# Impulse responses of a state-space layer from the outputs' powers, asked for five steps ahead

## The chip, the cores and the metric

One core of one Trainium2 chip runs one program. The metric is the time of one execution on the device, in microseconds (us), lower is better. Five engines matter: PE multiplies matrices (its weight loads are a row of their own, PEld), DVE is the vector engine, ACT the scalar engine, POOL a second vector engine (GpSimd), SP issues the transfers of weights.

## The reference

Three layers of a language model follow each other on 256 tokens of width 1024: a gated delta rule block with a dense feed-forward, an S5 block with a mixture of experts, and a block with pooling and neighbourhood attention. Only the S5 mixer is touched here. It is a diagonal complex state-space layer with 64 groups of 16 channels and 64 states per group:

```
u = x @ w_in
a_bar = exp(lam * dt)                       # one complex number per group and state
b_bar = ((a_bar - 1) / lam) * (b_re + i b_im)
h[t] = a_bar * h[t-1] + b_bar @ u[t]        # per group
y[t] = Re(c @ h[t]) + d_skip * u[t]
hid = gelu(y);  val, gate = split(hid @ w_glu);  out = val * sigmoid(gate)
```

Before it stands a layer norm, and after it another one and the mixture of experts.

## The kernel before

**Weights.** All weight matrices are streamed. SP loads raw pieces (`wr`), ACT copies a piece rounded to the fast matmul type (`wh`, line 290), DVE subtracts to get the rest (`wl`, line 292), and `mm3` (lines 336 to 338) makes each product of three matmuls.

**The S5 stage in blocks.** The 1024 channels are eight blocks k of 128 channels, that is of eight groups. Time is cut into 64 chunks of four steps (`CH = 4`). The chunk's own inputs reach its outputs through an impulse response of four taps, a 128 by 128 matrix per tap (`BD`, masked to the 16 by 16 diagonal squares with `bd16`). What came earlier reaches it through the states at the chunk's start. Real and imaginary parts lie in the two halves of the 128 partitions.

**Four kinds of work per block.** `maps(k)` makes the block's matrices: it transposes B (input vectors times powers 0 to 3 of a_bar) into `BT` (lines 1258 and 1259), multiplies each of the four powers in B with the output vectors CX to get the taps (`pk`, line 1265), masks them on DVE into `BD` (line 1267), and then has POOL write the output vectors times powers 1 to 4 over B, in place (`C`, lines 1275 to 1277: product, product, sum). `states(k)` turns the inputs by chunks (1286, 1291), multiplies with `BT` (`px`, 1301), and computes the 64 chunk states: products with the phases CC and SS on POOL (1308) and DVE (1309, 1310), a sum (1312), a scan (1313), and the products back on POOL (1317) and DVE (1318, 1319); line 1323 writes the states H over CC. `outputs(k)` multiplies H with C (`pyi`, 1335), adds the taps (`yp`, 1344) and the turned states (1346), adds the skip (1348, DVE), applies gelu (1350, ACT) and splits the result `hid` (330 on ACT, 331 on DVE). The products with `w_glu` (`po`) take `hid` block by block.

**The order of the work.** These parts are generators. `spawn(gen, lag)` queues one to go on after `lag` ticks; `tick` is called after each quarter of a weight piece, so four ticks are one block. Where a generator yields a number, it goes on that many ticks later; `S5L` holds these lags (`per=4`: a new block each four ticks, `m=1` and `mb=2` for maps). `flow` spawns states, maps and outputs at fixed ticks. The maps of blocks 0 and 1 are run at once, before the second half of the layer norm's result is turned to features (`to_features`: transposes at line 832, copies at 837 and 838). The tile framework then orders each engine's instructions; each engine works its list in order.

**Buffers.** `BD` of blocks 0 and 1 has its own two buffers, that of later blocks takes one of three slots of `BDs`. `bx` and `by`, the scaled input vectors (lines 1179 to 1188), share one temporary tile that is gone after B is built.

Of the kernel before, what the change touches and what calls it, by code (L numbers as in the profile page):

```python
# [11 lines left out]
F32 = mybir.dt.float32  # L12
# [4 lines left out]
ALU = mybir.AluOpType  # L17
# [22 lines left out]
BUFS = 5  # L40
EXTRA = 2
LAG = dict(nb=6, d=5, dp=4, n=1, rk=3, ks=4, kp=4, inv=7, i0=3, iy=8, i1=2, i2=1, lv=4, rq=4, qs=8, qp=2, v=2)
S5L = dict(per=4, s0=3, m=1, o=0, mb=2, a=2, b=2, c=2, d=4, e=2, f=1, g=1, ct=4, gt=4, keep=2)
MO = dict(d=3, t=2, b=5, a=2, sc=1)
WARM = dict(a=12, b=9, c=20, e=5, f=0)
MAGIC = 12582912.0
CH = 4
# [156 lines left out]
class Kern:  # L204
# [890 lines left out]
    def s5_tables(self, P, Pt):  # L1095

        nc, a = self.nc, self.a
        TT, TS, STT = nc.vector.tensor_tensor, nc.vector.tensor_scalar, nc.vector.scalar_tensor_tensor
        G = nc.gpsimd
        AR = P.tile([128, CH + 1, 64], F32, name="AR")  # L1100
        AI = P.tile([128, CH + 1, 64], F32, name="AI")
        nAI = P.tile([128, CH + 1, 64], F32, name="nAI")
# [2 lines left out]
        CC = P.tile([128, 64, NJ], F32, name="CC")  # L1105
        SS = P.tile([128, 64, NJ], F32, name="SS")
        CX = P.tile([128, 64, 16], F32, tag="CX", name="CX")
        self.s5t = (AR, AI, nAI, rad, B, CC, SS, CX)
        flat = B.rearrange("p k g c n -> p (k g c n)")
        wt, rbx, rby = (flat[:, n * 1024:n * 1024 + 1024].rearrange("p (g c) -> p g c", c=16) for n in (0, 2, 3))  # L1110

# [64 lines left out]
        TS(nfi, fi, -1.0, None, op0=ALU.mult)  # L1176
        yield 2
        wide = lambda v: v.unsqueeze(2).to_broadcast([128, 64, 16])
        bxy = Pt.tile([128, 2, 64, 16], F32, tag="gb", name="bxy")
        bx, by = bxy[:, 0], bxy[:, 1]  # L1180
        TT(bx, rbx, wide(fr), op=ALU.mult)
        TT(wt, rby, wide(fs), op=ALU.mult)
        yield 2
# [49 lines left out]
    def s5(self, tables):  # L1233
# [1 line left out]
        ctx = ExitStack()  # L1235
        P = ctx.enter_context(tc.tile_pool(name="s5", bufs=1))
        P2 = ctx.enter_context(tc.tile_pool(name="s52", bufs=2))
        AR, AI, nAI, rad, B, CC, SS, CX = self.s5t
        TT, TS, STT = nc.vector.tensor_tensor, nc.vector.tensor_scalar, nc.vector.scalar_tensor_tensor
        GT = nc.gpsimd.tensor_tensor  # L1240
        MM, TR = nc.tensor.matmul, nc.tensor.transpose
# [10 lines left out]

        def maps(k):

            BT = P2.tile([128, 4, 128], F32, tag="BT", name="BT", bufs=2)
            pt = self.bank("pbt", k < 2).rearrange("p (i f) -> p i f", i=4)
            for i in range(4):
                TR(pt[:, i, :], B[:, k, 2 * i:2 * i + 2].rearrange("p g c n -> p (g c n)"), ident)
            nc.scalar.activation(BT, pt, AF.Copy)
            bts[k] = BT  # L1260
            yield S5L["mb"]
            BD = P2.tile([128, CH, 128], F32, tag="BD", name="BD") if k < 2 else BDs[:, k % 3]
            pk = self.bank("pk", k < 2).rearrange("p (n f) -> p n f", n=CH)
            for n in range(CH):
                MM(pk[:, n, :], lhsT=B[:, k].rearrange("p g c n -> p (g c) n")[:, :, n],
                   rhs=CX[:, 8 * k:8 * k + 8, :].rearrange("p g c -> p (g c)"), start=True, stop=True)
            TT(BD, pk, bd16[:, None, :].to_broadcast([128, CH, 128]), op=ALU.mult)
            bds[k] = BD

            C = B[:, k].rearrange("p g c n -> p (g c n)").rearrange("p (g o c) -> p g o c", g=8, o=CH)  # L1270
            w = P2.tile([128, 8, CH, 16], F32, tag="cw", name="cw", bufs=1)
            g = slice(8 * k, 8 * k + 8)
            pw = lambda v: v[:, 1:CH + 1, g].rearrange("p n g -> p g n").unsqueeze(3).to_broadcast([128, 8, CH, 16])
            vec = lambda v: v[:, g, None, :].to_broadcast([128, 8, CH, 16])
            GT(C, pw(AR), vec(CX), op=ALU.mult)
            GT(w, pw(nAI), vec(CY), op=ALU.mult)
            GT(C, C, w, op=ALU.add)

        def states(k):

# [78 lines left out]
            nc.scalar.activation(uT[:, 0:4, 1:, js].rearrange("p k o j -> p k j o"),  # L1359
                                 self.turn4(f, 4).rearrange("p k (j o) -> p k j o", o=CH), AF.Copy)  # L1360
        for k in range(2):
            for _ in maps(k):
                pass
        nc.gpsimd.memset(R[:, :, 0], 0.0)
        self.to_features(self.src(1), 1)
        for t in range(2):
# [675 lines left out]
```

## Time and profile before

| | |
|---|---|
| runs shown: median (lowest to highest of 3) | 1286.02 us (1283.82 to 1287.36) |
| the profiled execution's own time | 1287.1 us |
| its span in the profile | 1285.3 us |
| busy share of the span: PE, PEld, DVE, ACT, POOL | 96%, 83%, 80%, 57%, 22% |
| granted TensorE clock, mean | 0.983 |
| S5 stage, from the last feed-forward product to the last gelu | about 405 to 532 us |

The page's busy shares are averages over stages with different limits. The stage touched here lasts about a tenth of the span, and what holds it up is read from the timelines of its engines. A row's duration runs from the engine's start on the instruction to its end, so time in which an instruction has started but is held up lies inside its duration. Consecutive rows of an engine overlap by some tens of nanoseconds.

### The profile page before, as it was taken

The numbers are of one execution on the slowest core, as the hardware profiler recorded it, in microseconds if no ns is written. First come the engines' busy times: TensorE is split into PE (matmuls) and PEld (weight loads), VectorE is DVE, ScalarE is ACT, GpSimd is POOL, SyncE is SP. The second block draws the span as 40 slices with busy tenths as digits, with TensorE's granted clock in tenths as the row PEclk, the third lists the DMA queues.
The fourth block names the chain that finished last, engine by engine and source line by source line (L and its number), as shares of the span: only waits on it lengthen the run. The fifth ranks groups of instructions, "written<-read, shape, count | busy, mean of one in ns | idle before, by whom it ended". The sixth has DMA issues, their size and how long they took to land. (4 is left out here: it accounts for less than half of the span.)

```text
span 1285.3 us, 19687 instructions
## 1 busy us (share of the span) xinstructions
PE 1229.9 (96%) x7579; PEld 1062.8 (83%) x7579; DVE 1031.8 (80%) x1507; ACT 732.3 (57%) x1086; POOL 280.1 (22%) x279
## 2 busy tenths in 40 slices
PE   8999998997999899889999999999999899999997
PEld 7999986997998777758888888888877677999886
DVE  6778879999767888678998999899979785766553
ACT  5744454442443653458777776867767465655442
POOL 2322001039996565110000000000002091000000
PEclk8998999999999999989999999999999899999999
DMA  8344224444644400337999989989977553545551
GB/s 330 132 140 140 78 88 162 153 176 163 244 177 159 147 34 34 124 130 269 343 343 329 341 316 372 331 319 374 346 294 301 185 184 131 194 171 193 189 186 51
DMA packets 44949, 269.18 MB, mean 209 GB/s; under 512 B 8880, under 2 KB 9280, under 8 KB 17968
## 3 DMA queue, kind: packets, MB, share of 16 engines
q1 hardware_dynamic: 40320, 257.12, 54.5%
q10 hardware_dynamic: 4336, 10.19, 2.3%
q8 instruction: 62, 1.02, 0.3%
q0 software_dynamic: 192, 0.54, 0.1%
q14 instruction: 39, 0.32, 0.1%
HBM read 266.51 MB, written 1.31 MB: 208 GB/s over the span
## 5 line engine op out<-in xcount | busy, mean ns | idle before, releaser
L292 DVE TENSOR_TENSOR wl<-wr,wh 128x1024 fp32r<-128x1024 f32 (+1 forms) x380 | 461.7, 1233 | 131.3 <-ACT wh L290 129.3
L290 ACT ACTIVATE wh<-wr 128x1024 fp32r<-128x1024 f32 (+2 forms) x390 | 391.2, 1025 | 233.1 <-PE po L338 84.9
L338 PE MATMUL pup<-wh,xg 128*128 128x512 f32 (+1 forms) x384 | 145.1, 378 | 3.4 <-PEq L1666 2.9
L337 PE MATMUL pup<-wl,xg 128*128 128x512 f32 (+1 forms) x384 | 146.3, 381 | 0.1
L336 PE MATMUL pup<-wh,xg 128*128 128x512 f32 (+1 forms) x384 | 146.1, 380 | 0.0
L292 DVE TENSOR_TENSOR wl<-wx,wh 128x1024 fp32r<-128x1024 f32 (+2 forms) x111 | 124.3, 1153 | 10.6 <-ACT wh L290 9.1
L290 ACT ACTIVATE wh<-wx 128x1024 fp32r<-128x1024 f32 (+1 forms) x112 | 104.9, 980 | 9.9 <-PE pup L338 5.9
L338 PE MATMUL p<-x,wl 128*128 128x256 f32 x320 | 91.6, 287 | 6.6 <-DVE wl L292 6.6
L292 POOL TENSOR_TENSOR wl<-wx,wh 128x1024 fp32r<-128x1024 f32 x1 | 2.5, 2478 | 409.8 <-ACT wh L290 409.8
L336 PE MATMUL p<-x,wh 128*128 128x256 f32 x320 | 91.3, 285 | 0.2 <-ACT s L994 0.2
L337 PE MATMUL p<-x,wh 128*128 128x256 f32 x320 | 91.0, 285 | 0.0
L338 PEld LDWEIGHTS pup<-wh,xg 128*128 128x128 f32 x384 | 72.6, 189 | 14.9 <-issue 3.3
L337 PEld LDWEIGHTS pup<-wl,xg 128*128 128x128 f32 x384 | 72.7, 189 | 13.8 <-DVE wl L292 3.5
L336 PEld LDWEIGHTS pup<-wh,xg 128*128 128x128 f32 x384 | 72.6, 189 | 10.9 <-issue 0.2
L337 PE MATMUL pdn<-wl,eh 128*128 128x512 f32 x176 | 70.0, 398 | 0.8 <-DVE wl L292 0.8
L336 PE MATMUL pdn<-wh,eh 128*128 128x512 f32 x176 | 69.8, 397 | 0.0
L338 PE MATMUL pdn<-wh,eh 128*128 128x512 f32 x176 | 69.5, 395 | 0.0
L338 PEld LDWEIGHTS p<-x,wl 128*128 128x128 f32 x320 | 61.8, 194 | 8.1 <-DVE wl L292 8.0
L336 PE MATMUL pm<-x,wh 128*128 128x256 f32 x224 | 63.5, 283 | 0.0
L338 PE MATMUL pm<-x,wl 128*128 128x256 f32 x224 | 63.4, 283 | 0.0
L337 PE MATMUL pm<-x,wh 128*128 128x256 f32 x224 | 63.4, 283 | 0.0
L336 PEld LDWEIGHTS p<-x,wh 128*128 128x128 f32 x320 | 62.0, 194 | 0.6 <-ACT s L994 0.4
(561 smaller groups left out, 3096.0 us busy)
## 6 DMA issues: line engine op xcount, KB each, us to landing
wr<-w_e SPq DMA_DIRECT2D x59, 1024.0 KB, 6.8
wx<-w_e SPq DMA_DIRECT2D x37, 1024.0 KB, 6.8
wr<-w_f SPq DMA_DIRECT2D x33, 1024.0 KB, 4.8
wr<-w_e SPq DMA_DIRECT2D x29, 768.0 KB, 5.1
wr<-w_up SPq DMA_DIRECT2D x16, 1024.0 KB, 4.6
wr<-w_dn SPq DMA_DIRECT2D x16, 1024.0 KB, 4.7
wx<-w_e SPq DMA_DIRECT2D x19, 768.0 KB, 6.0
wr<-w_glu SPq DMA_DIRECT2D x8, 1024.0 KB, 4.5
```

The lines of the kernel that those rows point to most:

```text
L290: self.hi = nc.scalar.activation(hi[:, :w], src, AF.Copy)
L292: self.los[self.n_split] = eng.tensor_tensor(lo[:, :w], src, hi[:, :w], op=ALU.subtract)
L336: mm(out, lhsT=l1, rhs=r1, start=start, stop=False)
L337: mm(out, lhsT=l1, rhs=r2, start=False, stop=False)
L338: self.mm = mm(out, lhsT=l2, rhs=r1, start=False, stop=stop)
```

## The change

The taps are computed from other operands. Tap n is the output vectors times power n times the input vectors. Before, the power was taken from B (stationary operand: every fourth element of B, four loads). Now the stationary operand is `bx`, the input vectors at power 0, contiguous and the same for all taps; the moving operand is CX for tap 0 and the first three powers of C for taps 1 to 3, in one matmul of 384 columns. So the taps now need C, and C is written over B as soon as B has been transposed. The second half of `maps` comes five ticks after the first in place of two. The first halves of blocks 0 and 1 still run at the stage's start, their second halves are spawned with lags of 10 and 13 ticks. All blocks take a slot of `BDs`, and `bx` gets a tile of its own that lives through the stage.

```diff
-S5L = dict(per=4, s0=3, m=1, o=0, mb=2, a=2, ...
+S5L = dict(per=4, s0=3, m=1, m0=10, o=0, mb=5, a=2, ...
...
+        bx = P.tile([128, 64, 16], F32, name="bx")
...
-        bxy = Pt.tile([128, 2, 64, 16], F32, tag="gb", name="bxy")
-        bx, by = bxy[:, 0], bxy[:, 1]
+        by = Pt.tile([128, 2, 64, 16], F32, tag="gb", name="by")[:, 0]
...
             nc.scalar.activation(BT, pt, AF.Copy)
             bts[k] = BT
-            yield S5L["mb"]
-            BD = P2.tile([128, CH, 128], F32, tag="BD", name="BD") if k < 2 else BDs[:, k % 3]
-            pk = self.bank("pk", k < 2).rearrange("p (n f) -> p n f", n=CH)
-            for n in range(CH):
-                MM(pk[:, n, :], lhsT=B[:, k].rearrange("p g c n -> p (g c) n")[:, :, n],
-                   rhs=CX[:, 8 * k:8 * k + 8, :].rearrange("p g c -> p (g c)"), start=True, stop=True)
-            TT(BD, pk, bd16[:, None, :].to_broadcast([128, CH, 128]), op=ALU.mult)
-            bds[k] = BD
...
             GT(C, pw(AR), vec(CX), op=ALU.mult)
             GT(w, pw(nAI), vec(CY), op=ALU.mult)
             GT(C, C, w, op=ALU.add)
+            yield S5L["mb"]
+            BD = BDs[:, k % 3]
+            pk = self.bank("pk").rearrange("p (n f) -> p n f", n=CH)
+            first = bx[:, g, :].rearrange("p g c -> p (g c)")
+            MM(pk[:, 0, :], lhsT=first, rhs=CX[:, g, :].rearrange("p g c -> p (g c)"), start=True, stop=True)
+            MM(pk[:, 1:, :].rearrange("p n (g c) -> p n g c", g=8), lhsT=first,
+               rhs=C[:, :, 0:CH - 1, :].rearrange("p g o c -> p o g c"), start=True, stop=True)
+            TT(BD, pk, bd16[:, None, :].to_broadcast([128, CH, 128]), op=ALU.mult)
+            bds[k] = BD
...
         for k in range(2):
-            for _ in maps(k):
-                pass
+            m = maps(k)
+            next(m)
+            self.spawn(m, S5L["m0"] + 3 * k)
```

How this moves instructions is seen in the program's order on three engines. The line numbers of the changed kernel differ a little: its 1268, 1269 and 1270 are the three operations on C (1275, 1276 and 1277 before), 1278 is the mask of the taps (1267 before), and from `states` on each line stands two further down.

POOL, two neighbouring blocks in the middle of the stage. Before:

```order
L1308 TENSOR_TENSOR p<-X,CC 128x512
L1317 TENSOR_TENSOR p<-X,CC 128x512
L1275 TENSOR_TENSOR B<-AR,CX 128x512
L1322 MEMSET CC 128x8
L1277 TENSOR_TENSOR B<-B,cw 128x512
L1276 TENSOR_TENSOR cw<-nAI,CY 128x512
L1308 TENSOR_TENSOR p<-X,CC 128x512
L1317 TENSOR_TENSOR p<-X,CC 128x512
```

Now:

```order
L1310 TENSOR_TENSOR p<-X,CC 128x512
L1268 TENSOR_TENSOR B<-AR,CX 128x512
L1270 TENSOR_TENSOR B<-B,cw 128x512
L1269 TENSOR_TENSOR cw<-nAI,CY 128x512
L1319 TENSOR_TENSOR p<-X,CC 128x512
L1324 MEMSET CC 128x8
L1310 TENSOR_TENSOR p<-X,CC 128x512
```

The three operations on C stood behind the second of the two state products (1317); now they stand between the two (1310 and 1319 of the changed kernel).

DVE, one block at the same place. Before:

```order
L331 TENSOR_TENSOR hid<-h,hid 128x256
L1309 TENSOR_TENSOR q<-X,SS 64x512
L1310 TENSOR_TENSOR q<-X,SS 64x512
L1312 TENSOR_TENSOR q<-p,q 128x512
L292 TENSOR_TENSOR wl<-wr,wh 128x1024
L1313 SCALAR_TENSOR_TENSOR X<-BDs,q 128x512
L1318 TENSOR_TENSOR q<-X,SS 64x512
L1319 TENSOR_TENSOR q<-X,SS 64x512
L1267 TENSOR_TENSOR BDs<-pk,cg 128x512
L1323 TENSOR_TENSOR CC<-p,q 128x8x63
L1348 SCALAR_TENSOR_TENSOR uT<-uT,sm,yp 128x256
```

Now:

```order
L331 TENSOR_TENSOR hid<-h,hid 128x256
L1311 TENSOR_TENSOR q<-X,SS 64x512
L1312 TENSOR_TENSOR q<-X,SS 64x512
L1314 TENSOR_TENSOR q<-p,q 128x512
L292 TENSOR_TENSOR wl<-wr,wh 128x1024
L1278 TENSOR_TENSOR BDs<-pk,cg 128x512
L1315 SCALAR_TENSOR_TENSOR X<-BDs,q 128x512
L1320 TENSOR_TENSOR q<-X,SS 64x512
L1321 TENSOR_TENSOR q<-X,SS 64x512
L1325 TENSOR_TENSOR CC<-p,q 128x8x63
L1350 SCALAR_TENSOR_TENSOR uT<-uT,sm,yp 128x256
```

Only the mask of the taps moved, from behind the scan's products to ahead of the scan; the number of operations is the same.

PE, at the start of the stage, where the last feed-forward products end and the first half of the normed tokens is turned to features. Before:

```order
L1258 MATMUL pbt<-cg,B 128x128 x4
L1265 MATMUL pk<-CX,B 128x128 x3
L832 MATMUL ptr<-cg,x 128x128 x4
L1265 MATMUL pk<-CX,B 128x128
L832 MATMUL ptr<-cg,x 128x128 x4
L1258 MATMUL pbt<-cg,B 128x128 x4
L1265 MATMUL pk<-CX,B 128x128 x4
L336 MATMUL ptf<-wh,x_70 128x512
```

Now:

```order
L338 MATMUL po<-wh,h_4168 128x512
L1259 MATMUL pbt<-cg,B 128x128 x8
L832 MATMUL ptr<-cg,x 128x128 x8
L336 MATMUL ptf<-wh,x_70 128x512
L337 MATMUL ptf<-wl,x_70 128x512
```

The taps of blocks 0 and 1 are gone from here; on PE they now stand among the products of the later input blocks (`pu`), behind the fourth and the tenth group of three of these, ahead of the first product of states (`px`). In the later blocks the taps stand ahead of `pyi`, four operations earlier than before.

## Rows read from the trace of the kernel before

**Rows 1.** Busy time by window (length; PE, PEld, DVE, ACT, POOL; clock, transfers).
```profile
435.00:466.00 31.00, 25.30 (x195) 22.30 (x194) 30.32 (x29) 13.68 (x24) 18.88 (x15) 0.94 0.14 55
466.00:514.00 48.00, 46.38 (x341) 38.04 (x339) 41.71 (x45) 21.84 (x41) 28.63 (x24) 1.00 0.12 45
```

**Rows 2.** Timeline of DVE, one block's period: start, duration, operation, [idle before, releaser].
```profile
491.15 1.04 DVE L331 TENSOR_TENSOR hid<-h,hid 128x256 fp32r<-128x256 f32 x1 [1.19 <-ACT hid L330]
492.22 1.66 DVE L1309 TENSOR_TENSOR q<-X,SS 64x512 f32<-64x512 f32 x1
...
495.30 1.22 DVE L292 TENSOR_TENSOR wl<-wr,wh 128x1024 fp32r<-128x1024 f32 x1
496.43 1.22 DVE L1313 TENSOR_TENSOR_SCAN X<-BDs,q 128x512 f32<-128x512 f32 x1
...
498.38 1.66 DVE L1319 TENSOR_TENSOR q<-X,SS 64x512 f32<-64x512 f32 x1
500.08 0.69 DVE L1267 TENSOR_TENSOR BDs<-pk,cg 128x512 f32<-128x512 f32 x1
500.69 0.87 DVE L1323 TENSOR_TENSOR CC<-p,q 128x504 f32<-128x504 f32 x1
501.48 0.47 DVE L1348 SCALAR_TENSOR_TENSOR uT<-uT,sm,yp 128x256 f32<-128x256 f32 x1
```

**Rows 3.** Timeline of POOL over the same period.
```profile
490.80 1.11 POOL L1276 TENSOR_TENSOR cw<-nAI,CY 128x512 f32<-128x512 f32 x1
491.87 1.47 POOL L1308 TENSOR_TENSOR p<-X,CC 128x512 f32<-128x512 f32 x1
497.73 1.78 POOL L1317 TENSOR_TENSOR p<-X,CC 128x512 f32<-128x512 f32 x1 [4.39 <-DVE X L1313]
...
499.66 1.36 POOL L1275 TENSOR_TENSOR B<-AR,CX 128x512 f32<-128x512 f32 x1
```

**Rows 4.** Timeline of DVE, the splits at 422 us.
```profile
422.31 10.32 DVE L292 TENSOR_TENSOR wl<-wr,wh 128x1024 fp32r<-128x1024 f32 x5 [1.52 <-ACT wh L290]
```

**Rows 5.** Timeline of POOL beside them.
```profile
423.06 2.16 POOL L1277 TENSOR_TENSOR B<-B,cw 128x512 f32<-128x512 f32 x1
```

**Rows 6.** Timeline of DVE, the last block's period.
```profile
513.47 0.47 DVE L1348 SCALAR_TENSOR_TENSOR uT<-uT,sm,yp 128x256 f32<-128x256 f32 x1
...
515.67 0.69 DVE L1309 TENSOR_TENSOR q<-X,SS 64x512 f32<-64x512 f32 x1
516.37 1.67 DVE L1310 TENSOR_TENSOR q<-X,SS 64x512 f32<-64x512 f32 x1
```

**Rows 7.** Groups of PE's weight loads by form, 395 to 530 us: busy, mean ns | idle.
```profile
L1265 PEld LDWEIGHTS pk<-CX,B 128*128 128x128 f32 x64 | 15.6, 325 | 1.8 <-DVE uT L1348 1.5
...
L1344 PEld LDWEIGHTS yp<-uT,BDs 128*128 128x128 f32 x48 | 8.0, 202 | 0.7
```

**Rows 8.** Timeline of PE, the first wait for a state, and one period.
```profile
446.91 1.52 PE L1335 MATMUL pyi<-B,CC 128*64 128x64 f32 x16 [3.67 <-DVE CC L1323]
...
494.97 1.90 PE L1265 MATMUL pk<-CX,B 128*128 128x128 f32 x8
...
496.71 1.37 PE L1344 MATMUL yp<-uT,BDs 128*128 128x256 f32 x8
```

**Rows 9.** Timeline of DVE where the layer norm ends.
```profile
406.76 1.40 DVE L872 SCALAR_TENSOR_TENSOR x<-lnr,lnrs,gb 128x512 f32<-128x512 f32 x2
...
409.82 1.28 DVE L838 TENSOR_TENSOR x<-ptr,x 128x512 fp32r<-128x512 f32 x2
```

**Rows 10.** Timelines of POOL and PE there.
```profile
408.84 2.02 POOL L1275 TENSOR_TENSOR B<-AR,CX 128x512 f32<-128x512 f32 x1 [5.74 <-DVE lnr L850]
...
405.86 0.60 PE L1258 MATMUL pbt<-cg,B 128*128 128x128 f32 x4
...
411.80 0.40 PE L338 MATMUL ptf<-wh,x 128*128 128x512 f32 x1
...
417.78 1.32 PE L832 MATMUL ptr<-cg,x 128*128 128x128 f32 x8 [0.80 <-DVE x L872]
```

More of the change, by code (lines that the diff above doesn't have):

```diff
@@ L42 @@
 LAG = dict(nb=6, d=5, dp=4, n=1, rk=3, ks=4, kp=4, inv=7, i0=3, iy=8, i1=2, i2=1, lv=4, rq=4, qs=8, qp=2, v=2)
-S5L = dict(per=4, s0=3, m=1, o=0, mb=2, a=2, b=2, c=2, d=4, e=2, f=1, g=1, ct=4, gt=4, keep=2)
+S5L = dict(per=4, s0=3, m=1, m0=10, o=0, mb=5, a=2, b=2, c=2, d=4, e=2, f=1, g=1, ct=4, gt=4, keep=2)
 MO = dict(d=3, t=2, b=5, a=2, sc=1)
@@ L1107, in s5_tables @@
         CX = P.tile([128, 64, 16], F32, tag="CX", name="CX")
-        self.s5t = (AR, AI, nAI, rad, B, CC, SS, CX)
+        bx = P.tile([128, 64, 16], F32, name="bx")
+        self.s5t = (AR, AI, nAI, rad, B, CC, SS, CX, bx)
         flat = B.rearrange("p k g c n -> p (k g c n)")
@@ L1237, in s5 @@
         P2 = ctx.enter_context(tc.tile_pool(name="s52", bufs=2))
-        AR, AI, nAI, rad, B, CC, SS, CX = self.s5t
+        AR, AI, nAI, rad, B, CC, SS, CX, bx = self.s5t
         TT, TS, STT = nc.vector.tensor_tensor, nc.vector.tensor_scalar, nc.vector.scalar_tensor_tensor
```

## The prediction

> **What bounds the kernel now.** The first view is the busy time by window, to find the stage's limit. From 466 to 514 us, four blocks, PE is busy 46.38 of 48 us and DVE 41.71 [rows 1]. That looks like PE, but a busy PE is not a PE that others wait for, so the second view is DVE's timeline over one block's period. It runs from one skip operation (L1348) to the next, 12.0 us: the one at 501.48 and that at 513.47 [rows 2, 6]. Inside it DVE is idle once, 1.19 us ahead of L331, for `hid` from ACT, which comes out of DVE's own L1348 through gelu. It never waits for PE. So DVE sets the pace, with a list it works in order.
>
> The third view, POOL's timeline beside it [rows 3], shows what DVE's time is made of. L1309 takes 1.66 us where POOL runs L1308 [rows 2, 3], and 0.69 where POOL isn't working [rows 6]. DVE starts it at 492.22; POOL's operation ends at 493.34, and 0.55 us later the DVE operation is over. So the one sits out the other. The same is read off L1319 beside L1317 (1.66), L331 beside L1276 (1.04) and L1323 beside L1275 (0.87) [rows 2, 3]. L1267, whose `pk` lies in PSUM, takes 0.69 though L1275 runs beside it [rows 2, 3]. POOL is held up in its turn: 1.47 or 1.78 us against the 1.11 of L1276 [rows 3]. So a POOL product of 128 by 512 costs a DVE operation with two operands in SBUF about 1.0 us, unless it falls on DVE's idle time or on an operation that reads PSUM.
>
> Who goes first when both have work queued? At 422 us five splits of DVE stand against POOL's operations on C. The five take 10.32 us, 2.06 each, where one alone takes 1.22 [rows 2, 4], and POOL's take 2.16 [rows 5]. They alternate, and each POOL operation costs DVE some 0.85 to 1.0 us.
>
> By the Trainium skill (SBUF — State Buffer, section "Who interferes with whom") a DVE instruction with two SBUF inputs contends with a GpSimd instruction that reads SBUF, and whoever issues first holds the pair for the whole instruction. It does not say who follows when both wait; if DVE kept it from one operation to the next, rival C below would be the forecast.
>
> **The change, part by part.**
>
> *PE, taps.* One block's four taps are eight passes that take from 494.97 to 496.71, 1.74 us [rows 8]; their strided weight loads are 325 ns each against 202 for contiguous ones [rows 7]. The new form has four passes over the same 1024 columns. The nearest contiguous case, `yp`, moves 1408 columns in eight passes (twice 256, 192, 128 and 128) in 1.37 us [rows 8], so 1024 columns are 1.0 us. Saved: some 0.75 us per block. In the loop this is worth nothing, since DVE does not wait for PE; if it did, it would be rival B.
>
> The Trainium skill (TensorE: Matmul & The Clock Gate, section "LDWEIGHTS (loading the stationary operand)") makes a load's time depend on the number of columns alone. By it stride would cost nothing and even rival B would save nothing; the measured 325 against 202 ns decide against it here.
>
> *Start of the stage.* L1275 of blocks 0 and 1 waited for the taps on PE and began at 408.84 [rows 10]. (The profile names DVE as releaser; the program's operands say PE, which ended at the same time.) Now it needs only the transposes (405.86 for 0.60 [rows 10]), so it stands in the queue when DVE comes to the two norm steps L872, 0.7 us each with two SBUF operands [rows 9]. By alternation each gets 1.0 us longer. L838 then starts 2.0 us later than 409.82 [rows 9], and the first L338, which needs it, at about 412.6 in place of 411.80 [rows 10]: +0.8. Behind it DVE gets back 0.8 us, by rows 4 (a split no longer meets the second L1275), and one L1267 of 0.6 that stood between the second norm's root and its L872. PE's next transposes, which wait for that L872 [rows 10], come about 0.7 us later. I take **+0.7**; bounds: -1.4 if DVE keeps the right of way (the first L338 then comes right behind the first L838, at 410.5), +2.0 if nothing is given back.
>
> *Taps of blocks 0 and 1.* They ran while PE had to wait for the normed tokens anyway. Now they stand among PE's `pu` products, ahead of the first `px`, where PE is the engine that others wait for. Two times 1.0, less a short wait of PE that they cover: **+1.9**; bounds 1.5 (0.75 each, if the two passes of 384 columns overlap their loads wholly) and 3.4 (if the moving operand with runs of 16 elements streams as slowly as the strided loads, 1.74 each).
>
> *Filling the pipeline, 435 to 466 us.* POOL's three operations on C of block 2 now come right behind the first products of block 1, beside L1309, L1310 and L1323 of DVE: +3.0 before the first state is out. PE waits there for L1323 already, 3.67 us [rows 8], and waits longer. What C cost here before: the 29 DVE operations of this window would take 21.7 us at their free durations (15 products and sums of 0.69, three scans and two splits of 1.22, three L1323 of 0.68, two masks, two L1348, L331, the end of a split); DVE is busy 30.3 [rows 1], so 8.6 are collisions, of which six state products make 5.8 and C some 2.9. Now block 2 costs 3.0 and block 3 1.0 to 2.0, since L1348 and the mask, which read PSUM, cover one or two of its three; one mask fewer falls here, -0.7. So 3.3 to 4.3 in place of 2.9, less what overlaps between neighbouring rows count twice: **+0.6**; bounds -0.2 and +2.5 (PE's late work, at the lower clock after the longer wait, holding up L1348 and the mask).
>
> *Full periods.* Three (blocks 4 to 6 on POOL) have all three C operations. Now, from the end of L1348: 4.1 us to the end of L1310, as in the last period, where POOL has no C operation (513.94 to 518.04) [rows 6]. Then alternate: C product 1.0, L1312 0.65, C sum 1.0, split 1.15 [rows 2]. The next C product runs beside the mask (0.65 of its 1.0). The scan takes 1.22 [rows 2]. L1318, POOL's state product and L1319 take 0.7, 1.0 and 0.65, L1323 0.65 and L1348 0.45. Sum 13.2, or 13.6 if the scan must wait for that C product too, which no row shows, since POOL always waits for the scan. Against 12.0: +1.2 to +1.6, I take 1.4, three times: **+4.2**. What is given back is in it: L331 and L1323 no longer collide (0.6 and 0.2 less). The bounds are 0 (DVE keeps the right of way) and 2.2 each (all three C operations cost a full 1.0, less the 0.8 given back).
>
> *The last two periods.* The fourth period has two C operations and no third: **+1.2** (0 to 1.4). The last gets a mask that used to lie one period earlier: **+0.7** (its row is 0.69 [rows 2]).
>
> Transfers, ACT's work and the arithmetic of `bx` and `by` are the same in number. The transfers are busy 0.12 of the time in this stage [rows 1], held by buffers, so the following stage has nothing in stock with which to make up for a late start.
>
> Sum: 0.7 + 1.9 + 0.6 + 4.2 + 1.2 + 0.7 = 9.3 us. On the profiled execution's 1287.1 (span 1285.3 and 1.8 around it, which nothing here touches) that is 1296.4; the median shown is 1286.0, 1.1 lower, so I forecast **1295.3**. The bounds, added, are +0.6 and +16.6, but they would hardly all fall on one side.
>
> **Rivals.** A measurement of this kernel can tell about 0.3%, 3.9 us, from no change.
>
> *B, faster: PE is the bound.* PE's window is 97% busy [rows 1], so it could be PE that sets the 12 us. Then 0.75 us times eight blocks, 6 us, go, and the stage's start is 1.2 us shorter: 1279, on the median's scale. It decides if DVE's waits turn out to end with PE. Against it: DVE's only wait is on its own result by way of ACT, and PE's wait ahead of `pyi` is for DVE [rows 8]. Chance 0.11.
>
> *C, no change: DVE keeps the right of way.* If POOL's operations on C had to wait for gaps of DVE (POOL now has nothing to do while DVE waits for gelu, but its next operation needs that same result), DVE's list would cost the same. The front would give -1.4 and the two taps +1.9: 1286.5. Against it: rows 4 and 5 show taking turns. Chance 0.13.
>
> *D, slower still: PE's lower clock.* PE now waits some 3.5 us in one piece in each period. The window with the one wait of 3.67 us [rows 8] has a mean granted clock of 0.94, the next one, without, 1.00 [rows 1]: 0.06 of 31 us are 1.9 us of PE lost per such wait. If three of these get onto the path: 5.6 more, 1301. Against it: in a full period PE would be done with `yp` some 4 us before DVE needs it. Chance 0.06.
>
> *The forecast*, 0.70.
>
> **How the numbers follow.** The forecast's own bounds, taken as mixed, reach from 1290 to 1299: the square root of the summed squares of the terms' distances from their bounds is 5.4 us downward and 3.7 upward. To leave no more than 2 in 10 out, the range takes in rival C and D and leaves out B and the extremes: 1286.5 to 1301. Slower by over 0.3%: forecast and D, 0.76. Within: C, 0.13. Faster: B, 0.11.
>
> **What would show it.** Right: in DVE's timeline the period is 13 to 13.7 us; L1314 (the sum) and the split, in the middle of it, take about 1.65 and 2.2 us each time; L331 takes 0.43 and the operation on H 0.68; POOL's row shows its C operations beside them, and no idle time ahead of the second state product to speak of. L872 at the stage's start takes about 1.7 us twice. PE's taps take about 1.0 us, and PE's waits for `hid` grow to over 3 us per block. Wrong: L1314 and the split keep 0.69 and 1.22 while POOL's operations on C grow (C), or the period falls below 12 us with DVE idle less (B). If the period is right and the time is not, the following stage took up the delay, which I think excluded.

## The result and the profile after

| | before | changed |
|---|---|---|
| median of 6 runs (lowest to highest) | 1286.14 us (1282.48 to 1288.30) | 1299.12 us (1294.74 to 1301.31) |
| ratio, 95% interval | 1 | 1.0096 (1.0078 to 1.0113) |
| the profiled execution's own time, span | 1287.1, 1285.3 us | 1300.55, 1298.6 us |
| granted TensorE clock, mean of the span | 0.983 | 0.971 |

The change made the kernel 13 us slower. The forecast was 1295.3, the range 1286.5 to 1301.0. Two tables by window (length; PE, PEld, DVE, ACT, POOL busy; clock, share and rate of transfers) say where the time went. The kernel before:

```profile
0.00:405.00 405.00, 383.68 (x2961) 352.74 (x2962) 332.40 (x637) 190.44 (x322) 165.97 (x178) 0.98 0.46 165
405.00:532.00 127.00, 114.49 (x798) 96.93 (x797) 109.81 (x116) 60.07 (x103) 66.04 (x50) 0.97 0.22 79
532.00:1285.30 753.30, 731.71 (x3823) 613.15 (x3822) 589.61 (x756) 481.77 (x663) 48.14 (x51) 0.99 0.69 255
```

The changed kernel, cut at about the same places of the program:

```profile
0.00:405.00 405.00, 383.61 (x2961) 352.74 (x2962) 332.35 (x637) 190.33 (x322) 165.57 (x178) 0.98 0.46 165
405.00:545.00 140.00, 119.95 (x768) 95.91 (x767) 117.17 (x116) 61.18 (x103) 68.78 (x50) 0.87 0.20 72
545.00:1298.60 753.60, 731.59 (x3822) 613.60 (x3820) 589.83 (x756) 481.07 (x663) 48.60 (x51) 0.99 0.69 255
```

All but some 0.7 us of it lies in the stage that was touched (12.6 of the span's 13.3 us, by the table of pieces below), and nothing of it came back behind. DVE is busy 7.4 us longer there with the same number of operations (x116). In the first and the last window, which have the same work, all is alike.

DVE's timeline over one full period of the changed kernel, from one skip to the next (the counterpart of [rows 2]):

```profile
488.40 0.43 DVE L331 TENSOR_TENSOR hid<-h,hid 128x256 fp32r<-128x256 f32 x1 [1.19 <-ACT hid L330]
...
489.64 1.67 DVE L1312 TENSOR_TENSOR q<-X,SS 64x512 f32<-64x512 f32 x1
491.42 1.41 DVE L1314 TENSOR_TENSOR q<-p,q 128x512 f32<-128x512 f32 x1
492.75 2.28 DVE L292 TENSOR_TENSOR wl<-wr,wh 128x1024 fp32r<-128x1024 f32 x1
494.96 0.68 DVE L1278 TENSOR_TENSOR BDs<-pk,cg 128x512 f32<-128x512 f32 x1
495.56 1.53 DVE L1315 TENSOR_TENSOR_SCAN X<-BDs,q 128x512 f32<-128x512 f32 x1
...
499.59 0.68 DVE L1325 TENSOR_TENSOR CC<-p,q 128x504 f32<-128x504 f32 x1
500.19 0.47 DVE L1350 SCALAR_TENSOR_TENSOR uT<-uT,sm,yp 128x256 f32<-128x256 f32 x1
```

POOL's timeline beside it (the counterpart of [rows 3]):

```profile
488.99 1.77 POOL L1310 TENSOR_TENSOR p<-X,CC 128x512 f32<-128x512 f32 x1 [3.33 <-ACT X L1305]
490.73 1.55 POOL L1268 TENSOR_TENSOR B<-AR,CX 128x512 f32<-128x512 f32 x1
492.36 1.60 POOL L1270 TENSOR_TENSOR B<-B,cw 128x512 f32<-128x512 f32 x1
494.03 1.97 POOL L1269 TENSOR_TENSOR cw<-nAI,CY 128x512 f32<-128x512 f32 x1
497.17 1.77 POOL L1319 TENSOR_TENSOR p<-X,CC 128x512 f32<-128x512 f32 x1 [1.16 <-DVE X L1315]
```

The period is 13.45 us in place of 11.97. The sum L1314 takes 1.41 in place of 0.68, the split 2.28 in place of 1.22, and even the scan 1.53 in place of 1.22: each sits out one of POOL's operations on C. L331 and L1325 are back to 0.43 and 0.68, since POOL now has nothing to do there, and the mask L1278, which reads PSUM, doesn't notice POOL. That is the mechanism of the forecast.

The filling of the pipeline is where it was off. DVE's timeline there:

```profile
461.86 0.48 DVE L1350 SCALAR_TENSOR_TENSOR uT<-uT,sm,yp 128x256 f32<-128x256 f32 x1 [1.12 <-PE yp L1348]
...
463.31 0.69 DVE L1278 TENSOR_TENSOR BDs<-pk,cg 128x512 f32<-128x512 f32 x1 [0.97 <-PE pk L1276]
...
465.52 2.01 DVE L1315 TENSOR_TENSOR_SCAN X<-BDs,q 128x512 f32<-128x512 f32 x1
...
471.99 0.48 DVE L1350 SCALAR_TENSOR_TENSOR uT<-uT,sm,yp 128x256 f32<-128x256 f32 x1 [0.82 <-PE yp L1348]
...
475.45 0.69 DVE L1311 TENSOR_TENSOR q<-X,SS 64x512 f32<-64x512 f32 x1 [1.38 <-ACT X L1305]
```

PE's timeline, the first wait for a state (the counterpart of [rows 8]):

```profile
452.13 1.94 PE L1337 MATMUL pyi<-B,CC 128*64 128x64 f32 x16 [6.22 <-DVE CC L1325]
```

PE waits 6.22 us where it waited 3.67, and what follows runs at the lower of its two clocks (pyi 1.94 us in place of 1.52). In the filling DVE then waits three times for PE, and right behind it once for X, which ACT takes from PE's px.

For the experiments the stage is cut into pieces by rows of the same two timelines: **front**, from the start of the first L872 to the start of the first state product of DVE (q<-X,SS); **fill A**, from there to the start of the first pyi on PE; **fill B**, from there to the end of the second skip; and the six intervals between the ends of the next skips, of which the first four have operations on C in the changed kernel. The stage is their sum. The pieces of a row come from one profiled execution; the ratio compares all executions with those of the kernel before, run on the same chip. (The second interval, 13.45 us, repeats to 0.02 us in the five kernels that have its order.)

| kernel | front | fill A | fill B | six intervals | stage | ratio (95%) |
|---|---|---|---|---|---|---|
| before | 28.68 | 11.47 | 19.11 | 11.97, 11.97, 11.99, 11.99, 10.11, 7.81 | 125.1 | 1 |
| changed | 31.32 | 14.02 | 20.34 | 14.74, 13.45, 13.80, 13.13, 10.72, 6.19 | 137.7 | 1.0096 (1.0078, 1.0113) |
| old taps | 32.32 | 14.02 | 20.56 | 15.25, 13.47, 13.81, 13.18, 10.71, 6.21 | 139.5 | (not to be compared) |
| C behind | 31.75 | 11.50 | 19.47 | 12.10, 12.56, 12.56, 12.57, 11.21, 6.21 | 129.9 | 1.0050 (1.0031, 1.0070) |
| front alone | 28.90 | 14.02 | 20.42 | 14.73, 13.47, 13.81, 13.16, 10.70, 6.39 | 135.6 | 1.0079 (1.0064, 1.0094) |
| memsets | 31.80 | 11.47 | 18.23 | 11.41, 11.34, 11.70, 11.34, 10.72, 6.21 | 124.2 | 0.9992 (0.9977, 1.0006) |
| both places | 28.84 | 11.47 | 19.48 | 13.05, 12.58, 12.56, 12.56, 11.24, 6.20 | 128.0 | 1.0028 (1.0014, 1.0043) |
| warm | 31.74 | 14.00 | 20.58 | 15.60, 13.47, 13.82, 13.12, 10.72, 6.21 | 139.3 | 1.0121 (1.0099, 1.0142) |
| blocks 2, 3 | 30.53 | 11.48 | 19.49 | 14.47, 13.45, 13.79, 13.14, 10.70, 6.21 | 133.3 | 1.0061 (1.0046, 1.0076) |
| old order | 28.80 | 11.47 | 21.30 | 12.09, 12.55, 12.56, 12.58, 10.72, 6.21 | 128.3 | 1.0035 (1.0021, 1.0049) |
| mask back | 29.07 | 11.47 | 20.74 | 13.49, 11.95, 11.96, 12.40, 10.74, 7.76 | 129.6 | 1.0016 (1.0002, 1.0029) |
| products on DVE | 29.44 | 11.29 | 17.14 | 12.68, 12.45, 12.45, 12.06, 7.34, 7.58 | 122.4 | 0.9994 (0.9980, 1.0007) |
| all on DVE | 29.43 | 8.67 | 19.03 | 12.79, 8.34, 11.19, 11.19, 11.19, 9.00 | 120.8 | 0.9977 (0.9962, 0.9991) |
| before, all on DVE | 29.29 | 8.61 | 19.63 | 12.66, 12.74, 14.40, 13.41, 12.05, 9.06 | 131.9 | 1.0061 (1.0045, 1.0077) |

### The profile page after: what moved, and what is told of

The parts are those of the page before. It is cut to its first block, busy times and chain, and to the rows that moved or that the text cites. A ratio compares the mean times of both kernels' runs of the same rounds, so it can differ in the third digit from the quotient of the medians.

```text
span 1298.6 us, 19625 instructions
## 1 busy us (share of the span) xinstructions
PE 1235.2 (95%) x7547; PEld 1062.2 (82%) x7547; DVE 1039.3 (80%) x1507; ACT 732.6 (56%) x1086; POOL 282.9 (22%) x279
## 5 line engine op out<-in xcount | busy, mean ns | idle before, releaser
L292 DVE TENSOR_TENSOR wl<-wx,wh 128x1024 fp32r<-128x1024 f32 (+2 forms) x111 | 124.2, 1152 | 10.8 <-ACT wh L290 9.1
```

The lines of the kernel that those rows point to most:

```text
L292: self.los[self.n_split] = eng.tensor_tensor(lo[:, :w], src, hi[:, :w], op=ALU.subtract)
```

## The experiments

**Old taps.** Is it the taps on PE (rival B) or POOL's products on C?

```diff
-            MM(pk[:, 0, :], lhsT=first, ...
-            MM(pk[:, 1:, :]..., lhsT=first, ...
+            for n in range(CH):
+                MM(pk[:, n, :], lhsT=B[:, k].rearrange("p g c n -> p (g c) n")[:, :, n],
+                   rhs=CX[:, 8 * k:8 * k + 8, :].rearrange("p g c -> p (g c)"), start=True, stop=True)
```

> The changed kernel with the taps made as before, by four matmuls with a strided stationary operand, in the changed order. The operand now holds C, so the taps are not the layer's. Port theory (DVE's pace is set by what POOL's products on C cost it): the form of the taps matters only twice, ahead of the first px, 2 x 0.75 = 1.5 us at most: 1299 to 1301, full periods 13 to 14.7 as in the changed kernel. Rival B (PE sets the pace): 8 x 0.75 = 6 us more, 1305.

The run took 2079 us. Other values come out of the stage, and the program behind it branches on loaded values (L1668), so only the stage can be compared. There the intervals are those of the changed kernel to within 0.05 us, except the first (15.25 against 14.74). The front is 1.0 us longer, where the expectation had up to 1.5, but that compares two clocks: PE ran slower at the stage's start of the changed kernel's profiled execution (0.83 between 405 and 425 us, here 1.00). The run "blocks 2, 3" below has the new taps and needs the same 12.72 us from the first L872 to the third L838 as this one; against its front of 30.53 the old taps cost 1.8 us. So the taps' form is worth something only where PE is waited for, at the stage's start and in the first interval. Rival B, 0.75 us in each block, is refuted for this kernel.

**C behind.** Operations on C of blocks 2 to 7 go behind the second state product again.

```diff
             bts[k] = BT
+            if k > 1:
+                yield 2
...
-            GT(C, pw(AR), vec(CX), op=ALU.mult)
-            GT(w, pw(nAI), vec(CY), op=ALU.mult)
-            GT(C, C, w, op=ALU.add)
-            yield S5L["mb"]
+            with tc.issue_after(self.prod2.ins) if k > 1 else nullcontext():
+                GT(C, pw(AR), vec(CX), op=ALU.mult)
+                GT(w, pw(nAI), vec(CY), op=ALU.mult)
+                GT(C, C, w, op=ALU.add)
+            yield S5L["mb"] - (2 if k > 1 else 0)
...
-            GT(p, X, CC[:, gs, :], op=ALU.mult)
+            self.prod2 = GT(p, X, CC[:, gs, :], op=ALU.mult)
```

(`issue_after` keeps an operation behind the named one on its engine; `prod2` is the second state product.)

> The changed kernel with one thing undone: C of blocks 2 to 7 stands on POOL behind the second state product again. Port theory: full periods back to 12.0 us (L1314 0.7, the split 1.2 again), the filling back to some 31 us, and only the start's and the taps' 2.7 us stay: 1289. Clock theory (what was underestimated is the lower clock that PE brings from the start and the longer waits): periods back to 12, but the filling stays at 33 or more: 1291 to 1293. If C's place doesn't matter: 1299.

Measured 1291.89. This one edit takes back 7.8 of the stage's 12.6 us. The filling is at 30.97 us (11.50 + 19.47), against 30.58 before and 34.36 in the changed kernel, although the front kept its low clock (0.83 between 405 and 425 us, as in the changed kernel). That speaks against the clock theory as far as it starts at the front. But the intervals stay at 12.56 where the port theory had said 12.0. Half a microsecond in each was not understood; the runs "old order" and "mask back" below settle it.

**Front alone.** C of blocks 0 and 1 goes behind the clearing of uT on POOL.

```diff
-        nc.gpsimd.memset(uT[:, :, 0, :], 0.0)
+        cleared = nc.gpsimd.memset(uT[:, :, 0, :], 0.0)
...
+            with tc.issue_after(cleared.ins) if k < 2 else nullcontext():
```

(the second around the three operations on C)

> The changed kernel with C of blocks 0 and 1 held behind the clearing of uT on POOL, so that it no longer meets the two norm steps L872 at the stage's start. Port theory: L872 back to 1.40 for the pair, the start shorter by 1.7 us, everything behind it unchanged: 1297.4. Clock theory: PE's clock also stays up between 410 and 416 us and the filling loses some of its 34.4 us: 1295 to 1296. If L872 was not on the path: 1299.

Measured 1295.45. The changed kernel at the stage's start, in DVE's timeline:

```profile
406.79 3.10 DVE L872 SCALAR_TENSOR_TENSOR x<-lnr,lnrs,gb 128x512 f32<-128x512 f32 x2
...
420.80 0.69 DVE L838 TENSOR_TENSOR x<-ptr,x 128x512 fp32r<-128x512 f32 x1 [2.01 <-ACT x L837]
```

POOL's timeline there (the counterpart of [rows 10]):

```profile
406.56 2.78 POOL L1268 TENSOR_TENSOR B<-AR,CX 128x512 f32<-128x512 f32 x2 [3.44 <-PE pbt L1259]
```

DVE's timeline of this experiment at the same place:

```profile
406.02 1.40 DVE L872 SCALAR_TENSOR_TENSOR x<-lnr,lnrs,gb 128x512 f32<-128x512 f32 x2
...
417.04 0.69 DVE L838 TENSOR_TENSOR x<-ptr,x 128x512 fp32r<-128x512 f32 x1 [0.72 <-ACT x L837]
```

The collision with L872 is as forecast: 3.10 us for the pair, 1.40 without [rows 9]. From the first L872 to the third L838 it is 14.01 us in the changed kernel, 11.02 here, 12.34 before. Of these 3.0 us the collision is 1.7 (3.10 less 1.40), and the rest goes with PE's clock, which stays up here as the clock theory had said: the run "blocks 2, 3" keeps the collision, has a shorter fall of the clock, and needs 12.72 us, 1.70 more than this run. 2.4 us of the 3.0 arrive at the first state product (31.32 against 28.90). The rest of the stage didn't notice: the filling is 34.44, with the clock at 1.00 up to 425 us. So the filling's loss does not come from the clock at the start.

**Memsets.** In place of its three operations on C of blocks 2 to 7 POOL writes the same three tiles and reads nothing; C of these blocks is left uncomputed.

```diff
-            GT(C, pw(AR), vec(CX), op=ALU.mult)
-            GT(w, pw(nAI), vec(CY), op=ALU.mult)
-            GT(C, C, w, op=ALU.add)
+            if k < 2:
...
+            else:
+                for d in (C, w, C):
+                    nc.gpsimd.memset(d, 0.5)
```

> The changed kernel with POOL's three products on C of blocks 2 to 7 replaced by memsets of the same tiles in the same places: POOL writes as much and reads nothing, and C of these blocks is left uncomputed. Port theory (shared reads): L1314 0.69, the split 1.22 and the scan 1.22 again, the four periods with C some 11 us each in place of 13.1 to 14.7, the filling some 3 us shorter: 1284 to 1287. If any work of POOL holds DVE up, or the pace comes from something else: periods over 12.5 and 1295 or more.

Measured 1284.54. DVE's timeline:

```profile
483.12 0.69 DVE L1318 TENSOR_TENSOR q<-p,q 128x512 f32<-128x512 f32 x1
483.73 1.22 DVE L292 TENSOR_TENSOR wl<-wr,wh 128x1024 fp32r<-128x1024 f32 x1
...
485.46 1.22 DVE L1319 TENSOR_TENSOR_SCAN X<-BDs,q 128x512 f32<-128x512 f32 x1
```

POOL's:

```profile
482.41 1.11 POOL L1274 MEMSET B<- 128x512 f32 x2
```

The intervals are 11.34 to 11.70. Not all writes stayed in their places: those of w wait for nothing, and all six run ahead at the stage's start, beside a split of DVE. POOL's row and DVE's there:

```profile
430.94 3.44 POOL L1274 MEMSET cw<- 128x512 f32 x6
```

```profile
432.49 1.21 DVE L292 TENSOR_TENSOR wl<-wr,wh 128x1024 fp32r<-128x1024 f32 x1
```

So two DVE operations with two SBUF operands stand beside POOL's writing, and both keep their free durations: the sum, which starts while the second write of its period runs (0.69 us), and this split, which lies wholly beside the six (1.21; the changed kernel's split at that place, beside L1269, takes 1.52). The period's own split and its scan meet nothing of POOL in this run. It is POOL's reading that DVE pays for. The writes are also fewer in the period and shorter (0.52 us each), so the intervals alone don't separate reading from mere presence; these two rows do, and so does the mask, which reads PSUM and takes 0.68 us beside POOL's product L1269 in the changed kernel. The Trainium skill says just that (SBUF — State Buffer, section "Who interferes with whom"): two SBUF inputs on DVE contend with a GpSimd instruction that reads SBUF, and not with one that only writes it. The trace agrees, 0.69 and 1.21 us. By the same rule the scan, with two SBUF inputs, was bound to be hit too, and it is: 1.53 us in the rows of the changed kernel's period.

Fill B is the second thing to see in this run. It is 18.23 us with no reading by C at all, and 19.11 in the kernel before, 0.9 us more, though that kernel also has other taps and a higher clock (0.95 between 435 and 470 us, here 0.85). "C behind", with the same taps and the same 0.85, has 19.47, 1.2 us more. So C behind the second product costs some 0.9 to 1.2 us in the whole filling (fill A is 11.47 to 11.50 in all three). The rows of this run's two skips in the filling show why it is so little: DVE waits for PE at both.

```profile
458.78 0.48 DVE L1354 SCALAR_TENSOR_TENSOR uT<-uT,sm,yp 128x256 f32<-128x256 f32 x1 [0.89 <-PE yp L1352]
...
467.02 0.48 DVE L1354 SCALAR_TENSOR_TENSOR uT<-uT,sm,yp 128x256 f32<-128x256 f32 x1 [0.59 <-PE yp L1352]
```

**Both places.** The last two edits together.

> Both places undone: C of blocks 0 and 1 behind the clearing of uT, C of blocks 2 to 7 behind the second state product; the new taps and the contiguous operand stay. Port theory: the two losses are separate collisions, so the gains add: 1299.1 less 7.2 less 3.7, 1288, with DVE's list as in the kernel before. If the two losses have one cause (a later start that the pipeline hands on), no more than the better of the two: 1292.

Measured 1289.96. The gains add: the stage is 9.7 us shorter than the changed kernel's, 7.8 and 2.1 apart. So they are two separate collisions. It is still 2.9 us longer than before.

**Warm.** Is the low clock behind PE's wait of 6.22 us on the path? 24 matmuls on a tile of zeros go ahead of the first pyi.

```diff
+            if k == 0:
+                self.warm(24)
             py = self.bank("pyi").rearrange("p (g f) -> p g f", g=8)
```

> The changed kernel with 24 matmuls that nobody reads ahead of the first pyi, in PE's wait of 6.2 us. Clock theory (part of the filling's loss is PE at its lower clock behind that wait): the clock stays at 1.00 there, pyi of block 0 takes 1.1 to 1.5 us in place of 1.94, DVE's waits for yp (1.12 and 0.82) shrink: 1296.5 to 1298. Port theory alone: DVE sets the end of the filling anyway, 1299.

Measured 1301.41. PE's timeline:

```profile
444.40 5.37 PE L260 MATMUL warm<-zero 128*64 128x512 bf16 x24
...
451.82 1.12 PE L1339 MATMUL pyi<-B,CC 128*64 128x64 f32 x16 [2.05 <-DVE CC L1325]
...
467.94 0.76 PE L338 MATMUL po<-wh,hid 128*128 128x512 f32 x1 [3.17 <-DVE hid L331]
```

DVE's:

```profile
471.92 0.48 DVE L1352 SCALAR_TENSOR_TENSOR uT<-uT,sm,yp 128x256 f32<-128x256 f32 x1 [3.44 <-PE yp L1350]
```

The clock is kept behind the first wait (0.97 between 435 and 470 us in place of 0.80; pyi 1.12 us in place of 1.94), and nothing is won: fill B is 20.58 against 20.34, since the second yp stands on PE behind products that wait for DVE's L331, and PE fell back to the lower clock in that wait. So the clock behind the first wait doesn't set the end of the filling. What the filling would take at the full clock throughout, this run doesn't show. PE's timeline of "C behind" says more:

```profile
448.16 1.94 PE L1340 MATMUL pyi<-B,CC 128*64 128x64 f32 x16 [3.70 <-DVE CC L1328]
```

Its pyi is as slow as the changed kernel's, and its filling is nevertheless 3.4 us shorter: the bulk of the loss is C's place and not the clock.

**Blocks 2, 3.** C of these two alone behind the second state product (`k in (2, 3)` in place of `k > 1` in the edit above).

> The changed kernel with C of blocks 2 and 3 alone behind the second state product; blocks 4 to 7 stay. Port theory: only the filling changes, from 34.4 us back to some 31, and the first full period (14.74 with a wait for px) comes down to the 13.5 of the others, which stay at 13.4 to 13.8: 1294 to 1295. If the filling's loss comes from the start or the taps: 1299.

Measured 1292.59. The filling is back to 30.97 us, and the full intervals of the later blocks stay at 13.45, 13.79 and 13.14, as expected. So the filling's loss is C's place and the periods' loss is C's place, each by itself. (0.8 us of its gain lie in the front, which this run didn't touch: the clock fell for a shorter time there.) The first interval didn't come down as expected (14.47): here POOL has five operations on C in it, the sum of block 3, the three of block 4 and, run ahead, the second product of block 5.

**Old order.** As "both places", but the product of the imaginary parts (w) is free to run ahead, so that POOL's order in the loop is that of the kernel before.

```diff
+            back = lambda: tc.issue_after(self.prod2.ins if k > 1 else cleared.ins)
+            with back():
+                GT(C, pw(AR), vec(CX), op=ALU.mult)
             GT(w, pw(nAI), vec(CY), op=ALU.mult)
+            with back():
+                GT(C, C, w, op=ALU.add)
```

> The new taps and the contiguous operand alone: POOL's order in the loop is that of the kernel before, operation by operation (the run with both places undone still had C's second product one block later than before). Port theory: DVE's list is that of the kernel before, periods of 12.0, and the two taps ahead of px cost about what the shorter start gives back: 1285 to 1288. If the taps' form or the later mask itself costs, periods of 12.5 as in the run with both places undone, 1290.

Measured 1288.9, at 12.55 us per interval again: the port theory's 12.0 fails although POOL's list is the old one. DVE's timeline shows what is left:

```profile
487.64 1.66 DVE L1326 TENSOR_TENSOR q<-X,SS 64x512 f32<-64x512 f32 x1
489.41 1.41 DVE L1330 TENSOR_TENSOR CC<-p,q 128x504 f32<-128x504 f32 x1
```

The operation on H takes 1.41 us in place of 0.87 [rows 2]. Before, the mask stood ahead of it and ran beside POOL's first product on C without noticing it; the change has moved the mask away. (Fill B of 21.30 has another cause, a wait of 1.53 us of the mask for pk behind PE's lower clock.)

**Mask back.** The test of that reading, as a further edit to "old order".

```diff
-            TT(BD, pk, bd16[:, None, :].to_broadcast([128, CH, 128]), op=ALU.mult)
+            if k > 1:
+                yield 1
+            with tc.issue_after(self.late.ins) if k > 1 else nullcontext():
+                TT(BD, pk, bd16[:, None, :].to_broadcast([128, CH, 128]), op=ALU.mult)
...
-            TT(q[hi], X[lo], SS[lo, gs, :], op=ALU.mult)
+            self.late = TT(q[hi], X[lo], SS[lo, gs, :], op=ALU.mult)
```

(the second on the last state product of DVE)

> As the run with POOL's old order, and DVE's mask (the product on pk) of blocks 2 to 7 behind the second state products again, so that DVE's list in the loop is that of the kernel before; the new taps stay. Cover theory: in the old place the mask, which reads PSUM, covers POOL's first product on C; without it that product falls on the operation on H (1.41 us in place of 0.87), 0.57 us in each of four periods: periods back to 12.0, 1286.5. If the mask's place doesn't matter: periods of 12.5 and 1289.

Measured 1289.17 beside 1287.03 for the kernel before in these rounds. DVE's timeline:

```profile
488.63 0.69 DVE L1286 TENSOR_TENSOR BDs<-pk,cg 128x512 f32<-128x512 f32 x1
489.24 0.87 DVE L1333 TENSOR_TENSOR CC<-p,q 128x504 f32<-128x504 f32 x1
```

The operation on H is at 0.87 and two intervals are at 11.95 and 11.96: the cover theory holds in the period. The whole is only 2 us above the kernel before and not at the expected 1286.5, because DVE waits 1.57 us for yp at the end of the filling and 1.80 for X behind it, and the last interval is 7.76 again. Whether the late mask brings these waits, no run shows.

**Products on DVE.** If sharing costs more than the work, the bound engine should do the work itself. As "both places", and:

```diff
-            GT(p, X, CC[:, gs, :], op=ALU.mult)
+            TT(p, X, CC[:, gs, :], op=ALU.mult)
```

(twice)

> As the run with both places undone, and POOL's two products of a state are made on DVE. Port theory: a product costs DVE 0.69 us of its own and some 1.0 if POOL makes it, so each block gets 0.6 shorter; with nothing of POOL's left to wait for DVE, C's three products fall where they like, on chain or on waits: periods 11.0 to 12.0, 1281 to 1288. If DVE is bound by its own work and not by sharing, 1.4 us more in each of eight blocks: 1297 or more.

Measured 1284.89, no different from the kernel before, and 1.0% below the changed kernel. The intervals of 12.45 are above the 11.0 to 12.0 expected: C's products still meet DVE's (its own state product takes 1.76 there).

**All on DVE.** The same with C of blocks 2 to 7 on DVE too.

```diff
+            CT = GT if k < 2 else TT
...
-            GT(C, pw(AR), vec(CX), op=ALU.mult)
-            GT(w, pw(nAI), vec(CY), op=ALU.mult)
-            GT(C, C, w, op=ALU.add)
+                CT(C, pw(AR), vec(CX), op=ALU.mult)
+                CT(w, pw(nAI), vec(CY), op=ALU.mult)
+                CT(C, C, w, op=ALU.add)
```

> C of blocks 0 and 1 behind the clearing of uT; C of blocks 2 to 7 and both products of a state on DVE, POOL has none of them. Port theory: DVE's own list is 14 operations of 0.69 or less, a scan and a split of 1.22, the skip and the end of a split: 11.6 us and some 0.4 of gaps, its wait for gelu filled: periods of 12.0 in place of 13.1 to 14.7, although DVE has 3.5 us more work in each: 1286 to 1290. If sharing isn't what costs, periods of 15 and more and 1305.

Measured 1283.36. DVE's timeline, in part:

```profile
495.18 0.48 DVE L1354 SCALAR_TENSOR_TENSOR uT<-uT,sm,yp 128x256 f32<-128x256 f32 x1 [0.26 <-PE yp L1352]
495.58 0.69 DVE L1323 TENSOR_TENSOR p<-X,CC 128x512 f32<-128x512 f32 x1
496.29 0.69 DVE L1324 TENSOR_TENSOR q<-X,SS 64x512 f32<-64x512 f32 x1
...
497.69 0.69 DVE L1272 TENSOR_TENSOR B<-AR,CX 128x512 f32<-128x512 f32 x1
```

Every operation is at its free duration, the period is 11.19 us with five more operations in it, two products of a state and three on C, and the wait for gelu is filled. It is better than expected (12.0 us): that sum had gaps between the operations, where the rows follow each other at 0.60 to 0.71 us. DVE now waits for PE once a period. This version is faster than both kernels: 0.9977 of the time before, interval 0.9962 to 0.9991.

**Before, all on DVE.** What the change is worth where POOL is out of the way.

> The kernel before, with C of blocks 2 to 7 and both products of a state on DVE; the old taps and the old places stay. It asks what the new taps are worth once POOL no longer holds DVE up and PE is busy all but a microsecond of each period (11.19 us in the run with the new taps). If the taps' 0.75 us then lie on the path: periods of 11.5 to 12, 3 us over the run with all on DVE, 1286. If DVE still sets the pace: periods of 11.2 and the same 1283.

Measured 1293.48, 10 us above the version with the new taps, where 3 or none were expected. DVE's timeline:

```profile
489.25 0.48 DVE L1349 SCALAR_TENSOR_TENSOR uT<-uT,sm,yp 128x256 f32<-128x256 f32 x1 [0.95 <-PE yp L1347]
...
491.63 0.69 DVE L1309 TENSOR_TENSOR p<-X,CC 128x512 f32<-128x512 f32 x1 [1.30 <-ACT X L1304]
...
501.42 0.69 DVE L1267 TENSOR_TENSOR BDs<-pk,cg 128x512 f32<-128x512 f32 x1 [0.34 <-PE pk L1265]
```

DVE waits for PE in several places of each period. The two kernels differ in the taps' form, in the places of taps and C, and in DVE's order, and no run here parts these. What is shown is that the new form, with C behind the second state product, is 0.8% shorter than the old one (0.9977 against 1.0061) when POOL shares nothing in the loop.

## Why the prediction was right, and where it was not

The direction, the place and the mechanism were right: POOL's products on C, moved among DVE's operations with two SBUF operands, lengthen these, and by the run with memsets it is their reading. That the time stayed inside the range owes something to luck: the last interval gave back 1.6 us that no term had forecast. Without them the time would have been some 1300.7 us (an estimate, 1299.1 and 1.6), with the range's end at 1301.0. Rival C (DVE keeps the right of way) is refuted by L1314, the split and the scan; rival B by the old taps. The terms:

| term | predicted | measured | from |
|---|---|---|---|
| start of stage, and the taps of blocks 0 and 1 | +0.7 and +1.9 | +2.6 | front, 31.32 - 28.68 |
| filling | +0.6 (-0.2 to +2.5) | +3.8 | fill A and B, 34.36 - 30.58 |
| three full periods | +4.2 (0 to 6.6) | +6.1 | 2.77, 1.48 and 1.81 |
| fourth period | +1.2 | +1.1 | 13.13 - 11.99 |
| last period | +0.7 | +0.6 | 10.72 - 10.11 |
| last interval | 0 | -1.6 | 6.19 - 7.81 |
| sum | +9.3 | +12.6 | |

- **Start and taps**: the sum is right, in part by luck. At the third L838 the changed kernel is 1.7 us behind the kernel before (14.01 against 12.34), where 0.7 was taken, and the taps and what else lies on the way to the first state product add 1.0, not 1.9. In "blocks 2, 3", with the same start and a shorter fall of PE's clock, the two are 0.4 and 1.5 (12.72 and 30.53 in all). So both terms were somewhat too large, and the lower clock, which neither had, made up for it.
- **Filling**: the term that failed, outside its bounds. The price of what C costs now was about right: 2.55 us before the first state (14.02 against 11.47), where 3.0 was said, and 2.1 behind it (20.34 against 18.23 with memsets), where 1.0 to 2.0 was said. What failed is the subtraction: what C cost before, 2.9 us, was counted from DVE's busy time. Taking C's reading away wins only 0.9 us (19.11 against 18.23) to 1.2 us (19.47 against 18.23), since DVE then waits for yp (0.89 and 0.59 us at the two skips of the run with memsets). A collision ahead of such a wait costs only what goes beyond it, and its removal gives back no more.
- **Full periods**: two of three came out at 13.45 and 13.80, forecast 13.2 to 13.6; the second of these has 0.46 us of idle time ahead of L1325, which the profile puts down to DVE itself. The scan does need the port, which the prediction left open. The first, 14.74, has DVE waiting 1.38 us for px, which PE made late: rival D in one place. In the later periods PE falls to its lower clock too (0.87 between 502 and 516 us), but DVE never waits for it there.
- **Cover**: the prediction counted the mask as cover at its new place and missed what it had covered at the old one, some 0.6 us per period. That did not show in the forecast, since the period was added up anew, but it decides what undoing the move of C alone can bring (12.56 in place of 11.97).
- **Last interval**: not in the prediction at all. Before, PE waited 2.91 us ahead of the last pyi and ran slower behind it; now it waits 1.03. The window of that stretch in the kernel before:

```profile
525.00:532.00 7.00, 7.00 (x41) 6.01 (x40) 2.04 (x3) 1.60 (x4) 0.00 (x0) 0.76 0.00 0
```

and in the changed one:

```profile
538.00:545.00 7.00, 5.96 (x44) 5.24 (x44) 2.94 (x5) 2.88 (x5) 0.00 (x0) 1.00 0.00 1
```

The clock worked against rival D here: it is 1.00 in place of 0.76, in line with the 1.6 us less. No run changed this clock alone.

## What to carry to other kernels

Where an operation is moved on one engine, list what it stood beside and what it will stand beside on the engine that shares its port, and price the cover that goes as well as the collisions that come. What a collision gives back when it is removed is read from the next wait behind it, not from busy time. If a helper engine's operation costs the bound engine more (some 1.0 us here) than doing it there (0.7), the bound engine should do it: the loop with five more operations on DVE was the fastest.

## What was not expected of the hardware

The window around the stage's start in the changed kernel and in the run with the old taps, in that order:

```profile
405.00:425.00 20.00, 17.11 (x74) 13.16 (x73) 16.21 (x24) 9.42 (x15) 4.49 (x6) 0.83 0.38 132
```

```profile
405.00:425.00 20.00, 15.79 (x81) 12.10 (x80) 17.36 (x23) 10.80 (x16) 6.15 (x6) 1.00 0.45 156
```

PE has the same two waits there, 1.52 and 0.85 us ahead of the transposes, and in one execution the granted clock fell to 0.83 in the mean and in the other it stayed at 1.00. In the first the distance from L872 to the third L838 is 14.01 us, in the second 12.72. The run "blocks 2, 3", with the same two waits, lies between:

```profile
405.00:425.00 20.00, 17.67 (x83) 13.79 (x84) 17.34 (x22) 10.72 (x16) 6.57 (x7) 0.91 0.51 174
```

Its distance is 12.72 us as well. "C behind", "memsets" and "warm" have the waits, 0.83 and 14.38 to 14.43 us. So some 1.3 to 1.7 us of the start hang on how long the clock is down, and these waits alone do not decide that. The scan on DVE, 1.22 us alone, went up to 1.52 to 1.70 in full periods and to 2.01 in the filling beside POOL's products.
